# A batched matrix product on one core: the transposes of x in two pieces per half where there were four

## The chip, the core and the metric

The kernel runs on one core of one Trainium2 chip. Five engines work side by side and meet at semaphores: TensorE multiplies, VectorE, ScalarE and GpSimd copy and convert, SyncE (SP) starts the transfers between HBM and the on-chip memory (SBUF). Matrix products land in a second small memory (PSUM). The metric is the device time of the kernel in microseconds, lower is better. Before the change it is 132.26 us, the median of three runs from 132.15 to 132.43 us.

## The reference

```python
batch, dim_i, dim_j, dim_k = 32, 256, 512, 384
np.einsum('bij,bjk->bik', x, y).astype(np.float32)   # x: 32x256x512, y: 32x512x384, float32
```

Thirty-two independent products of a 256x512 matrix with a 512x384 matrix. Read are 16.8 MB of x and 25.2 MB of y, written are 12.6 MB.

## The kernel before, in words

The batches go in N = 8 groups of Q = 4. A group's four batches lie on four bands of 32 partitions each, and TensorE works on the bands as four tiles of 32 rows. One group's x is one load of 2 MB, its y one load of 3 MB, its output one store of 1.5 MB. x and y each have two buffers, so group n+2 is loaded into the place of group n.

- **SP** (lines 97 to 110) starts loads for groups 0 and 1 at once. Then, for n = 2 to 7, it waits until GpSimd has converted both halves of x of group n-2 and starts the load of x of group n; it waits for GpSimd's first half of x of group n-1 (by then y of group n-2 is converted too) and starts the load of y of group n. Only after the last load come the eight stores, in order, each behind a wait for the group's results; the last one waits for ScalarE's and VectorE's last copies. All transfers are in one queue.
- **GpSimd** (lines 118 to 133) converts x to 16 bits, half by half (a half e is four of the eight row blocks), then y in two or four pieces. Half e of x of group n waits for `s_free`, which VectorE raises with its first copy after a half's transposes; a piece of y waits until TensorE has used the piece that it overwrites.
- **VectorE** (lines 144 to 181) turns a half of x around into `xt_sb`, which holds one half at a time and is overwritten chunk by chunk. In `vector_half(n, e)` it transposes the half that comes next, while TensorE multiplies half (n, e): it waits for `chunk_done(n, e, a)`, TensorE's mark that chunk a of `xt_sb` has been read, and transposes piece a of the next half into that place. After the pieces it copies the last 5 of the half's 16 result blocks out of PSUM.
- **TensorE** (lines 220 to 240) does a half in 64 matmuls: 16 steps t, four bands each. `take` waits for a mark and takes it away. It takes one mark of `s_yr` and one of `s_xt` every four steps, which is once per chunk, and raises `s_pe` at each chunk's end.
- **ScalarE** (lines 185 to 199) copies the other 11 result blocks of each half.

The two halves of a group use different PSUM banks, so that TensorE can go on with one while the other is copied out. Nothing is planned by a scheduler: the order on every engine is that of the code.

Of the kernel before, what the change touches and what calls it, by code (L numbers as in the profile page):

```python
# [13 lines left out]
STEP = 4  # L14
# [4 lines left out]
def kernel(  # L19
# [14 lines left out]
    T = J // PQ  # L34
    TW = T // 2
    N = B // Q
    NC = T // STEP
# [21 lines left out]
    s_pe = nc.alloc_semaphore("s_pe")  # L59
# [27 lines left out]
    def chunk_done(n, e, a):  # L87
        return (n * NE + e) * MARKS + (a + 1 if a < NC - 1 else MARKS)
# [48 lines left out]


    v = nc.vector
    AW = STEP // 2  # L140
    words = x_r.bitcast(F32).rearrange("p e h (q t) -> p e t h q", t=TW)
    xt_w = xt_sb.rearrange("p t (h s) -> p t h s", s=PQ)

    def transpose_x(e, a):
        w = slice(a * AW, (a + 1) * AW)
        v.transpose(xt_w[:, w], words[:, e, w]).then_inc(s_xt, 1)  # L146
# [6 lines left out]
    def collect(copy, n, e, blocks, first=None, last=None):  # L153
        for i, (g, h) in enumerate(blocks):
            ins = copy(  # L155
                o_sb[g * PQ : (g + 1) * PQ, n, e, h],
                o_ps[h * PQ : (h + 1) * PQ, e * Q + g, :K],
            )
            if i == 0 and first is not None:
                ins.then_inc(first, 1)  # L160
            if i == len(blocks) - 1 and last is not None:
                ins.then_inc(last, 1)

    def vector_half(n, e):
        for a in range(NC):
            v.wait_ge(s_pe, chunk_done(n, e, a))
            if a == 0:
                v.wait_ge(s_cast, NE * n + e + 2)
            transpose_x(1 - e, a)
        collect(v.tensor_copy, n, e, BLOCKS[-OWN:], s_free, s_dve)  # L170

    v.sem_inc(s_dve, NE)
    v.wait_ge(s_cast, 1)
    for a in range(NC):
        transpose_x(0, a)
    with v.Fori(0, N - 1) as n:
        for e in range(NE):
            vector_half(n, e)
    vector_half(N - 1, 0)
    v.wait_ge(s_pe, chunk_done(N - 1, 1, NC - 1))  # L180
    collect(v.tensor_copy, N - 1, 1, BLOCKS[-OWN:], None, s_dve)
# [21 lines left out]
    def take(sem):  # L203
        te.wait_op(sem, 1, "sem-ge").then_inc(sem, -1)  # L204

    def product(ps, w, m, start, stop, g):
        return te.add_instruction(  # L207
            mybir.InstMatmult(
                name=nc.get_next_instruction_name(),
                start_tensor_calc=start,  # L210
                stop_tensor_calc=stop,
                tile_size=(PQ, P),
                tile_position=(PQ * g, 0),
                engine=mybir.EngineType.PE,
                ins=[te.lower_ap(m), te.lower_ap(w)],
                outs=[te.lower_ap(ps)],
            )
        )

    xt = xt_sb.bitcast(MM_DT).rearrange("p t (m c) -> p t m c", c=2)  # L220
    with te.Fori(0, N):
        with te.Fori(0, NE) as e:
            take(s_act)
            take(s_dve)
            for t in range(T):
                if t % STEP == 0:
                    take(s_yr)
                    take(s_xt)
                for g in range(Q):
                    s = slice(g * PQ, (g + 1) * PQ)  # L230
                    ins = product(
                        o_ps[:, e * Q + g, :K],
                        xt[s, t // 2, :, t % 2],
                        y_r[s, t],
                        t == 0,
                        t == T - 1,
                        g,
                    )
                    if t == T - 1 or (g == Q - 1 and t % STEP == STEP - 1):
                        ins.then_inc(s_pe, 1)  # L240
# [30 lines left out]
```

## Time and profile before

| | before |
|---|---|
| median of three runs | 132.26 us (132.15 to 132.43) |
| the profiled execution | 132.16 us, its span 130.8 us |
| busy VectorE / ScalarE / GpSimd | 82.7 / 84.3 / 74.2 us |
| busy TensorE matmul / weight load | 65.0 / 53.7 us |
| TensorE's mean granted clock | 0.798 |
| moved by DMA | 54.55 MB, mean 417 GB/s |
| transposes | 64, mean 625 ns |

Times in the profile count from the span's start. A row of the timeline names the start, the length, the engine, the line, the operation with the tile that it writes and reads, how many instructions are drawn together, and in brackets how long the engine had been idle and what ended that. `SPq` is SP's own instruction queue. The notes "<-DMA", "<-DVE" (VectorE), "<-POOL" (GpSimd) and "<-PE" (TensorE) name what a wait ended with.

### The profile page before, as it was taken

Reading aid. Unit: us, or ns where it says so; the run is one execution under the profiler, and the core shown is the slowest. Engines: PE = TensorE matmul, PEld = TensorE weight load, DVE = VectorE, ACT = ScalarE, POOL = GpSimd, SP = SyncE. Lnnn points to the kernel's source line nnn. Section 1 sums busy time; section 2 is a strip of 40 time slices with the busy share of each in tenths; the row PEclk is TensorE's granted clock in tenths of the full one; section 3 lists DMA queues with packets and bytes.
Section 4 is the critical chain, followed back from the end, with each engine's and each line's share of the span. In section 5 each row is a group of like instructions: output and inputs, shape, how many; then the busy total and the mean of one; then the engine's idle time right before and its main releaser. Section 6 shows DMA issues by size and latency. Waiting matters only on the chain. (4 is left out here: it accounts for less than half of the span.)

```text
span 130.8 us, 3204 instructions
## 1 busy us (share of the span) xinstructions
PE 65.0 (50%) x1024; PEld 53.7 (41%) x1024; DVE 82.7 (63%) x144; ACT 84.3 (64%) x178; POOL 74.2 (57%) x42
## 2 busy tenths in 40 slices
PE   0000069903991698099529915980985499100000
PEld 0000057702990575089329505970963387000000
DVE  0006005897379989966998997589989957920000
ACT  0400000899359989993999899489999967995000
POOL 0047195499919955992899469758964970000000
PEclk9999999996589779756986995599599558965555
DMA  5999999999999999999999999999999999999996
GB/s 105 421 461 406 426 433 466 406 423 436 458 393 431 433 466 398 421 438 458 396 456 413 458 391 453 413 431 421 458 413 405 427 427 428 432 425 428 436 425 263
DMA packets 3459, 54.55 MB, mean 417 GB/s; under 512 B 384, under 2 KB 384, under 8 KB 384
## 3 DMA queue, kind: packets, MB, share of 16 engines
q1 hardware_dynamic: 3456, 54.53, 98.2%
q14 instruction: 3, 0.02, 0.0%
HBM read 41.94 MB, written 12.58 MB: 417 GB/s over the span
## 5 line engine op out<-in xcount | busy, mean ns | idle before, releaser
L155 ACT COPY o_sb<-o_ps (+1 forms) x176 | 82.8, 470 | 31.7 <-PE o_ps L207 29.5
L207 PE MATMUL o_ps<-y_r,xt_sb 32*128 32x384 f16 x1024 | 65.0, 406 | 46.7 <-PEq L204 46.5
L207 PEld LDWEIGHTS o_ps<-y_r,xt_sb 32*128 32x128 f16 x1024 | 53.7, 112 | 57.7 <-issue 52.2
L146 DVE STREAM_TRANSPOSE xt_sb<-x_r 128x256 f32<-128x256 f32 x64 | 38.2, 625 | 31.0 <-PE o_ps L207 20.3
L132 POOL CAST y_r<-y_sb 128x1536 f16<-128x1536 f32 (+1 forms) x22 | 44.3, 2049 | 8.0 <-DMA y_sb<-in_y_dram 7.8
L155 DVE COPY o_sb<-o_ps 32x384 f32 (+1 forms) x80 | 44.5, 557 | 1.6
L124 POOL CAST x_r<-x_sb 128x2048 f16<-128x2048 f32 x16 | 30.2, 1893 | 24.6 <-PE o_ps L207 8.3
L192 ACT ACT_TABLE_LOAD x1 | 1.3, 1283 | 3.5 <-PEq L77 3.5
L255 POOL MEMSET const-float32-0.0<- 128x1 f32 x1 | 0.1, 98 | 0.2 <-issue 0.2
L192 ACT COPY spare<-const-float32-0.0 1x1 f32<-1x1 f32 x1 | 0.2, 190 | 0.0
L255 POOL MEMSET const-bfloat16-1.0<- 128x1 bf16 x1 | 0.1, 101 | 0.0
L255 POOL MEMSET const-uint8-127<- 128x1 uint8 x1 | 0.1, 101 | 0.0
L255 POOL MEMSET const-float32-1.0<- 128x1 f32 x1 | 0.1, 98 | 0.0
## 6 DMA issues: line engine op xcount, KB each, us to landing
y_sb<-in_y_dram SPq DMA_DIRECT2D x8, 3072.0 KB, 16.9
x_sb<-in_x_dram SPq DMA_DIRECT2D x8, 2048.0 KB, 17.4
out_dram<-o_sb SPq DMA_DIRECT2D x8, 1536.0 KB, 24.6
```

The lines of the kernel that those rows point to most:

```text
L124: po.tensor_copy(x_r[:, e], x_sb[n % 2][:, e * H : (e + 1) * H]).then_inc(s_cast, 1)
L132: ins = po.tensor_copy(y_r[:, s], y_sb[n % 2][:, s])
L146: v.transpose(xt_w[:, w], words[:, e, w]).then_inc(s_xt, 1)
L155: ins = copy(o_sb[g * PQ : (g + 1) * PQ, n, e, h], o_ps[h * PQ : (h + 1) * PQ, e * Q + g, :K],)
L192: a_.copy(spare, nc.const_aps.tensor(0.0, [1, 1], F32))
L207: return te.add_instruction(mybir.InstMatmult(name=nc.get_next_instruction_name(), start_tensor_calc=start, stop_tensor_calc=stop, tile_si ...
L255: nc = _bacc.Bacc("TRN2", target_bir_lowering=False, num_devices=1)
```

## The change

A half of x is transposed by two instructions of 128 partitions x 512 words, where it was four of 256 words. VectorE waits for TensorE's chunk 1 ahead of the first piece and for chunk 3 ahead of the second (before: for each of the chunks 0 to 3 ahead of its own piece). TensorE takes a mark of `s_xt` at steps 0 and 8 of a half, where it was 0, 4, 8 and 12. Marks of y, the marks that TensorE raises and all else stay as they are. Two lines more stand in the file, so line 146 becomes 147, 155 becomes 156, and TensorE's 207 becomes 208.

```diff
     v = nc.vector
-    AW = STEP // 2
+    PT = 2
+    AW = TW // PT
...
     def vector_half(n, e):
-        for a in range(NC):
-            v.wait_ge(s_pe, chunk_done(n, e, a))
+        for a in range(PT):
+            v.wait_ge(s_pe, chunk_done(n, e, (a + 1) * NC // PT - 1))
             if a == 0:
                 v.wait_ge(s_cast, NE * n + e + 2)
             transpose_x(1 - e, a)
...
     v.wait_ge(s_cast, 1)
-    for a in range(NC):
+    for a in range(PT):
         transpose_x(0, a)
...
             for t in range(T):
                 if t % STEP == 0:
                     take(s_yr)
+                if t % (T // PT) == 0:
                     take(s_xt)
```

## The prediction

> **What bounds the kernel now.** I read the busy times first, and then the transfers, since their row in the page is full from end to end. These are the first part of the page, the second (40 slices of 3.27 us, tenths of the 16 DMA engines' time), the third, and the sixth (transfers by line: count, size, median time to landing).
>
> ```profile
> PE 65.0 (50%) x1024; PEld 53.7 (41%) x1024; DVE 82.7 (63%) x144; ACT 84.3 (64%) x178; POOL 74.2 (57%) x42
> ...
> DMA  5999999999999999999999999999999999999996
> ...
> q1 hardware_dynamic: 3456, 54.53, 98.2%
> ...
> y_sb<-in_y_dram SPq DMA_DIRECT2D x8, 3072.0 KB, 16.9
> x_sb<-in_x_dram SPq DMA_DIRECT2D x8, 2048.0 KB, 17.4
> out_dram<-o_sb SPq DMA_DIRECT2D x8, 1536.0 KB, 24.6
> ```
>
> The one queue fills 98.2% of the span. No compute engine comes near that; the busiest, ScalarE, has 84.3 of 130.8 us. So the question is not what an engine saves but whether the queue ever waits for a release. For that I read the timeline at the places where GpSimd starts on a y (the end of the y load, where the bracket says so):
>
> ```profile
> 0.74 0.38 SPq L68 DMA_DIRECT2D x_sb<-in_x_dram  x1
> 8.46 3.72 POOL L124 CAST x_r<-x_sb 128x2048 f16<-128x2048 f32 x2 [8.01 <-DMA x_sb<-in_x_dram]
> 15.74 5.70 POOL L132 CAST y_r<-y_sb 128x1536 f16<-128x1536 f32 x4 [3.56 <-DMA y_sb<-in_y_dram]
> ...
> 40.45 5.44 POOL L132 CAST y_r<-y_sb 128x3072 f16<-128x3072 f32 x2
> 49.72 1.89 POOL L124 CAST x_r<-x_sb 128x2048 f16<-128x2048 f32 x1 [2.00 <-DVE o_sb L155]
> 52.41 5.44 POOL L132 CAST y_r<-y_sb 128x3072 f16<-128x3072 f32 x2 [0.80 <-DMA y_sb<-in_y_dram]
> 62.54 1.90 POOL L124 CAST x_r<-x_sb 128x2048 f16<-128x2048 f32 x1 [2.86 <-PE o_ps L207]
> 64.59 5.44 POOL L132 CAST y_r<-y_sb 128x3072 f16<-128x3072 f32 x2 [0.16 <-issue]
> 73.76 1.89 POOL L124 CAST x_r<-x_sb 128x2048 f16<-128x2048 f32 x1 [1.89 <-DVE o_sb L155]
> 76.79 5.44 POOL L132 CAST y_r<-y_sb 128x3072 f16<-128x3072 f32 x2 [1.14 <-DMA y_sb<-in_y_dram]
> 86.66 1.89 POOL L124 CAST x_r<-x_sb 128x2048 f16<-128x2048 f32 x1 [2.59 <-PE o_ps L207]
> 88.93 5.70 POOL L132 CAST y_r<-y_sb 128x1536 f16<-128x1536 f32 x4 [0.38 <-DMA y_sb<-in_y_dram]
> 97.53 1.89 POOL L124 CAST x_r<-x_sb 128x2048 f16<-128x2048 f32 x1 [1.06 <-DVE o_sb L155]
> 101.35 5.70 POOL L132 CAST y_r<-y_sb 128x1536 f16<-128x1536 f32 x4 [1.92 <-DMA y_sb<-in_y_dram]
> ```
>
> y of groups 0, 3, 5 and 7 lands at 15.74, 52.41, 76.79 and 101.35: 12.22, 12.19 and 12.28 us per group. One group's 5120 KB arrive every 12.2 us, whatever the engines do; x is 2048 of these 5120 KB, 4.9 us. After 101.35 the eight stores take the 29.45 us left, 3.68 us each.
>
> Next, how far ahead of need the transfers are started: SP's rows, the stores' line (first and last start), the loads' time to landing, and SP's last wait (in total, times, longest).
>
> ```profile
> 26.69 0.33 SPq L72 DMA_DIRECT2D y_sb<-in_y_dram  x1
> 35.74 0.33 SPq L72 DMA_DIRECT2D y_sb<-in_y_dram  x1
> 84.10 0.33 SPq L72 DMA_DIRECT2D y_sb<-in_y_dram  x1
> ...
> L95 SPq DMA_DIRECT2D out_dram<-o_sb x8: 332/430/434, 84.5 to 119.4; - x8
> ...
> DMA to landing us min/median/max: 7.7/17.4/20.6
> ...
> SPq L110 <- SPq L110: 11.0, 1, 11.0
> ```
>
> The load of y of group 2 starts at 26.69. The transfer ahead of it, x of group 2, ends at 15.74 + 12.2 + 4.9 = 32.8: 6.1 us of work still queued, the least of all loads. For y of group 3 it is 45.0 - 35.74 = 9.3 us, for y of group 7 it is 88.93 + 4.9 - 84.10 = 9.7 us. The last store starts at 119.4, and the store ahead of it ends at 130.8 - 3.68 = 127.1: 7.7 us. A start needs a lead: the very first x landed 7.7 us after its start, with 4.9 us of transfer, so at most 2.8 us. What a release may be late without cost is then 3.3 us at y of group 2, 6.5 us or more at the later loads and 4.9 us at the last store.
>
> **The change part by part.** (1) The piece. Transposes as they stand (their group with its busy time; then least, median and longest ns), four in a row, and the one at the end of group 3's first half with the copy and the TensorE work around it:
>
> ```profile
> L146 DVE STREAM_TRANSPOSE xt_sb<-x_r 128x256 f32<-128x256 f32 x64 | 38.2, 625 | 31.0 <-PE o_ps L207 20.3
> ...
> L146 DVE STREAM_TRANSPOSE xt_sb<-x_r x64: 592/640/649, 10.4 to 108.9; 128x256 f32<-128x256 f32 x64
> ...
> 10.38 2.21 DVE L146 STREAM_TRANSPOSE xt_sb<-x_r 128x256 f32<-128x256 f32 x4 [10.38 <-POOL x_r L124]
> ...
> 55.60 8.20 PE L207 MATMUL o_ps<-y_r,xt_sb 32*128 32x384 f16 x128 [3.78 <-PEq L204]
> 61.24 0.65 DVE L146 STREAM_TRANSPOSE xt_sb<-x_r 128x256 f32<-128x256 f32 x1 [0.50 <-PE o_ps L207]
> 61.91 2.86 DVE L155 COPY o_sb<-o_ps 32x384 f32 x5
> ```
>
> No row shows 512 words in one instruction. Four of 256 in a row take 2.21 us, 0.55 each, against 0.64 alone. If the length costs nothing, a piece takes 0.64; if the instruction is twice one alone, 1.28. I take one alone and one directly behind it, 0.64 + 0.55 = 1.19, because the rows in a row show that almost all of a transpose repeats with its words. VectorE's total: 32 x 1.19 = 38.1 us against the sum of 64 that was 38.2; nothing gained or lost there.
>
> (2) The release, the one loss. VectorE waits for chunk 3 with half the work still to do, where one quarter was left. The last piece ends 1.19 - 0.64 = 0.55 us later behind TensorE's half (between 0 and 0.64), and with it the first copy, `s_free`, GpSimd's second half of x and what SP queues behind that. Behind the longer wait on VectorE stand its five copies; TensorE waits for their mark only two halves later, and SP for the last ones. In the first groups this makes the start at 26.69 later by 0.55 us against 3.3 us that are free: cost 0.
>
> (3) Does the lateness pile up? GpSimd's round runs from the start on y to the end of the next x half, with TensorE's half and VectorE's last piece inside. From the rows: 49.72 + 1.89 - 40.45 = 11.16 us for group 2, then 12.03, 11.06, 11.76 and 10.49 for groups 3 to 6. With 0.55 more, groups 3 and 5 (12.58 and 12.31) exceed the 12.2 us of the transfers. Carried through: group 2 starts on y at 41.00, group 3 at 52.71 (0.30 late), group 4 at 65.29 (0.70), group 5 at 76.90 (0.11), group 6 at 89.21 (0.28), and its round ends at 100.25, ahead of y of group 7 at 101.35. So no load is started more than 0.70 + 0.55 = 1.25 us later, where at least 6.5 us are free, and the tail begins on time: cost 0.
>
> (4) TensorE's marks. 32 of 64 takes go; what one costs no row shows, between 0 and the 0.2 us that TensorE waited for transposes in all. The new danger is the second half of a group, which starts as the first ends, with half its `xt_sb` still being written. The fastest half takes 3.17 us (below, the row of that wait and of that half):
>
> ```profile
> PE o_ps L207 <- DVE xt_sb L146: 0.2, 1, 0.2
> ...
> 96.76 3.17 PE L207 MATMUL o_ps<-y_r,xt_sb 32*128 32x384 f16 x64 [0.56 <-PEq L204]
> ```
>
> Step 8 comes 1.58 us in, the piece is there after 1.19 (1.28 at most). No wait, and if there were one, the 3.78 us that TensorE idled ahead of 55.60 cover it: cost 0.
>
> (5) The tail, where cover is least.
>
> ```profile
> 108.81 10.61 ACT L155 COPY o_sb<-o_ps 32x384 f32<-32x384 f32 x22 [2.12 <-PE o_ps L207]
> 109.61 5.72 DVE L155 COPY o_sb<-o_ps 32x384 f32<-32x384 f32 x10
> ```
>
> The last store follows ScalarE's 22 copies, which end at 119.42 and depend on TensorE's banks. VectorE's ten end at 115.33, with the change at 115.9: 3.5 us ahead. Cost 0.
>
> Sum: 132.16 + 0 = 132.16 us for the profiled execution. The median shown is 0.10 us above it; I predict 132.2.
>
> **The rivals.** *Slower: the release round becomes the period.* Speaking for it: two of five rounds already pass 12.2 us with the change. With d for what a piece adds, group 2 starts on y at 40.45 + d, and five rounds later (56.50 + 5 d) the tail is late by 6 d + 40.45 + 56.50 - 101.35 = 6 d - 4.4 us. The last store has 4.9 us free, so a loss of 0.26 us needs d = 1.6, a piece of 2.25 us. Should a long piece cost twice the doubled one, 2.56 us (d = 1.92), the tail is 7.1 us late and the time 132.16 + 2.2 = 134.4. Against it: the rows of four, which grow no faster than the words.
>
> *Slower: GpSimd is shut out while VectorE transposes.* Each longer piece would then hold up a cast by 0.55 more; with three casts in a round d becomes 0.55 + 1.65 = 2.2, the tail is 8.8 us late, the time 136.1. The x casts speak against it (least, median, longest):
>
> ```profile
> L124 POOL CAST x_r<-x_sb x16: 1889/1893/1895, 8.5 to 97.5; 128x2048 f16<-128x2048 f32 x16
> ```
>
> They differ by 6 ns, and the second pair of halves at 8.46 took 3.72 us with the transposes of 10.38 running beside it. [...]
>
> *Faster: fewer instructions disturb the transfers less.* Ahead of most compute, y of group 0 came in 15.74 - 8.46 = 7.28 us; three fifths of 12.2 are 7.32. The 0.04 us over 13 such stretches (8 groups of 5 MB, 12 MB of stores) would be 0.5 us, 131.6, were all engines' work free of charge. VectorE's transposes are an eighth of the engines' busy time, and their words stay: 0.06 us at the most. [...]
>
> *The change doesn't do what it says*: the code fixes the counts (32 transposes, 32 marks of x), so they can't come out otherwise; it has no chance of its own.
>
> **How the numbers follow.** What can be told from no change is about 0.2%, 0.26 us: the three runs lie 0.28 us apart. No change 0.81; the slow round 0.06, the lock 0.01, an unseen slowing 0.05: slower 0.12; faster 0.07. Range: below to 131.9 (the runs' spread and half of the 0.5), above to 132.7, which is 0.5 us for a part of the lateness uncovered; the cases beyond, 134.4 and 136.1, stay out with the rest at under 2 in 10.
>
> **What would show it.** Transposes: 32, mean 1.10 to 1.28. The queue still at 98%, y of group 7 still ending GpSimd's wait at 101.3 to 101.4, rounds of GpSimd 0.5 longer, SP's load starts 0 to 1.3 later, its last wait still near 11 us. I am wrong if a "9" falls in the DMA row, if GpSimd's start on the last y no longer waits for DMA, or if the last wait falls toward 6 us.

## The result

The changed kernel takes 132.70 us in the median of 22 runs (132.44 to 133.06), the kernel before 132.49 us in 22 runs beside them (132.28 to 132.30 beside the later experiments); the ratio is 1.0022 with a 95% interval from 1.0013 to 1.0031. That is a small loss, about 0.3 us (0.17 to 0.41 by the interval), where the prediction was no change. One of the six runs of experiment 4 was in a slower state of the core and is left out of the figures given for it.

The profiled execution took 132.54 us, 0.38 us more than the profiled one of before. Its span is 130.8 us, the same as before. So these two differ only in what lies around the span: 1.36 us before, 1.74 us after. The page of the changed kernel (busy times, the DMA row in 40 slices, the queues):

```profile
PE 65.2 (50%) x1024; PEld 52.1 (40%) x1024; DVE 79.0 (60%) x112; ACT 84.1 (64%) x178; POOL 74.1 (57%) x42
...
DMA  5999999999999999999999999999999999999996
...
q1 hardware_dynamic: 3456, 54.53, 98.3%
q14 instruction: 2, 0.02, 0.0%
```

The transfers are as full as they were. One row differs that I had not read: queue 14 fetches instructions, and it moved two packets in the span. The page of the kernel before has three:

```profile
q14 instruction: 3, 0.02, 0.0%
```

The timeline of the changed kernel, at the places that the prediction named: SP's start of the load of y of group 2, GpSimd's starts on y of groups 2 to 7, VectorE's last copies.

```profile
27.24 0.33 SPq L72 DMA_DIRECT2D y_sb<-in_y_dram  x1
...
41.17 5.44 POOL L132 CAST y_r<-y_sb 128x3072 f16<-128x3072 f32 x2
52.47 5.44 POOL L132 CAST y_r<-y_sb 128x3072 f16<-128x3072 f32 x2
64.84 5.44 POOL L132 CAST y_r<-y_sb 128x3072 f16<-128x3072 f32 x2
76.89 5.44 POOL L132 CAST y_r<-y_sb 128x3072 f16<-128x3072 f32 x2 [0.68 <-DMA y_sb<-in_y_dram]
89.03 5.70 POOL L132 CAST y_r<-y_sb 128x1536 f16<-128x1536 f32 x4
101.56 5.70 POOL L132 CAST y_r<-y_sb 128x1536 f16<-128x1536 f32 x4 [1.70 <-DMA y_sb<-in_y_dram]
113.33 2.84 DVE L156 COPY o_sb<-o_ps 32x384 f32<-32x384 f32 x5 [0.34 <-PE o_ps L208]
```

And there the lines of the transposes and of the stores (least, median and longest ns, first and last start), and SP's last wait (in total, times, longest):

```profile
L147 DVE STREAM_TRANSPOSE xt_sb<-x_r x32: 1058/1104/1119, 10.5 to 109.0; 128x512 f32<-128x512 f32 x32
```

```profile
L95 SPq DMA_DIRECT2D out_dram<-o_sb x8: 332/430/439, 84.6 to 119.5; - x8
```

```profile
SPq L110 <- SPq L110: 10.9, 1, 10.9
```

Where the changed kernel lacks a fetch is seen in the stretch from 104 to 130 us (queue: packets, MB, share of 16 engines). The kernel before:

```profile
q1 hardware_dynamic: 1008, 10.92, 98.9%
q14 instruction: 1, 0.01, 0.1%
```

The changed kernel, with no row of queue 14 in the same stretch:

```profile
q1 hardware_dynamic: 1008, 10.92, 98.8%
```

### The profile page after: what moved, and what is told of

Same layout as the page of the kernel before. It is cut to its first block, busy times and chain, and to the rows that moved or that the text cites. A ratio compares the mean times of both kernels' runs of the same rounds, so it can differ in the third digit from the quotient of the medians.

```text
span 130.8 us, 3112 instructions
## 1 busy us (share of the span) xinstructions
PE 65.2 (50%) x1024; PEld 52.1 (40%) x1024; DVE 79.0 (60%) x112; ACT 84.1 (64%) x178; POOL 74.1 (57%) x42
## 3 DMA queue, kind: packets, MB, share of 16 engines
q1 hardware_dynamic: 3456, 54.53, 98.3%
## 5 line engine op out<-in xcount | busy, mean ns | idle before, releaser
L208 PEld LDWEIGHTS o_ps<-y_r,xt_sb 32*128 32x128 f16 x1024 | 52.1, 112 | 60.8 <-issue 55.3
L147 DVE STREAM_TRANSPOSE xt_sb<-x_r 128x512 f32<-128x512 f32 x32 | 34.5, 1096 | 35.2 <-PE o_ps L208 24.3
```

The source lines that it names most:

```text
L208: return te.add_instruction(mybir.InstMatmult(name=nc.get_next_instruction_name(), start_tensor_calc=start, stop_tensor_calc=stop, tile_si ...
```

## The experiments

Two theories stood against each other. A: the loss lies outside the span and comes from the length of VectorE's instruction stream, which went from 70 to 58 instructions. B: it lies inside, and comes from the longer pieces or the marks. Every run carries its time and its span (to 0.1 us), so the difference, called "outside" below, is a measurement of its own; a figure for it is the mean over the runs. A fetch is a packet of queue 14 of 8192 bytes, and a page is the stretch of instructions that one fetch brings. The counts of instructions are those of the stream as it stands in memory, where a loop's body counts once; the traces bear out the steps between them (VectorE's records hold 67 different instructions of before and 55 of the changed kernel, also 12 apart; experiment 3 has 12 instructions more at its waits).

**1. The kernel before, again.**

```diff
-    AW = STEP // 2
+    AW = STEP // 2  # words of t per piece
```

> The kernel before with a comment added and nothing else; it gives the spans of runs of the kernel before, of which only one is known (132.16 us with a span of 130.8, so 1.36 us outside). Theory A (the loss lies outside the span): the spans are those of the changed kernel, on the mean 131.0, and 1.3 to 1.4 us lie outside where the changed kernel has 1.67 to 1.76. Theory B (the loss lies inside the span, lost in the transfers): the spans are 0.2 to 0.3 us shorter than those of the changed kernel, about 130.75, and as much lies outside as there. Both: ratio to the kernel before 1.000.

Measured: 132.29 us, ratio 1.0000 (0.9991 to 1.0010). The mean span is 131.01 us, that of the 22 runs of the changed kernel is 131.01 us too. Outside lie 1.33 us here (1.28 to 1.38 in 12 runs) and 1.72 us there (1.67 to 1.76 in 22). The two do not overlap. So the loss lies outside the span, 0.39 us by these means, and B is left with nothing that shows.

**2. TensorE's marks alone, with four pieces.**

```diff
-        v.transpose(xt_w[:, w], words[:, e, w]).then_inc(s_xt, 1)
+        ins = v.transpose(xt_w[:, w], words[:, e, w])
+        if a % 2 == 1:
+            ins.then_inc(s_xt, 1)
...
-                    take(s_xt)
+                if t % (2 * STEP) == 0:
+                    take(s_xt)
```

> The kernel before with TensorE's part alone: VectorE keeps its four pieces and gives a mark with the second and the fourth, TensorE takes two marks per half. VectorE has the 70 instructions of the kernel before in its stream, TensorE has two fewer than before. Theory A in the form that VectorE's shorter stream makes the loss: 132.2 to 132.6, ratio 1.000, 1.3 to 1.4 outside. In the form that TensorE's shorter stream makes it: ratio 1.002 with 1.7 outside. Theory B (longer pieces): ratio 1.000.

Measured: 132.37 us, ratio 1.0002 (0.9989 to 1.0014), outside 1.33, three fetches in the span. Neither the missing takes nor a stream of TensorE that is two instructions shorter cost or gain anything that shows.

**3. Both parts of the change, with VectorE's stream filled up to 70.**

```diff
     v.wait_ge(s_cast, 1)
+    for _ in range(24):
+        v.wait_ge(s_cast, 1)
     for a in range(PT):
         transpose_x(0, a)
```

(In the built program the 24 waits stand as 12 instructions.)

> The changed kernel, with idle waits put on VectorE ahead of its first transposes (they are already met there and end microseconds before TensorE needs anything), so that its stream has the 70 instructions of the kernel before where the change left 58. Theory A (length of VectorE's stream): ratio 1.000, 1.3 to 1.4 us outside the span. Theory B (two long pieces cost inside): ratio 1.002 as the changed kernel.

Measured: 132.34 us, ratio 1.0000 (0.9988 to 1.0011), outside 1.33, mean span 131.02. From its page:

```profile
q14 instruction: 3, 0.02, 0.0%
...
L147 DVE STREAM_TRANSPOSE xt_sb<-x_r 128x512 f32<-128x512 f32 x32 | 34.5, 1097 | 34.8 <-PE o_ps L210 22.8
```

The transposes are those of the changed kernel, 32 of 1.1 us; the third fetch is back in the span, and the loss is gone. The change as it works on the data costs nothing that these runs can tell (the interval is 0.12% to either side).

**4. One piece, filled up to 70.**

```diff
-    PT = 2
+    PT = 1
...
+    for _ in range(36):
+        v.wait_ge(s_cast, 1)
```

> One piece of 1024 words per half and one mark, VectorE's stream again at 70 instructions. The release comes about 2.1 - 0.64 = 1.5 us later per half than before, where the change made it 0.5. Theory A: the same time as before or within 0.1 us, since 6 x 1.5 - 4.4 = 4.6 us of lateness at the tail stays under the 4.9 us that I had free; 1.3 to 1.4 outside. Theory B: the loss inside the span grows with the delay, from 0.3 to about 0.9 us, ratio near 1.007.

Measured: 139.72 us (138.62 to 140.27 in five runs), ratio 1.0572 (1.0544 to 1.0600), outside 1.37. My sum for this run was wrong by far. Its DMA row, its timeline and the line of its stores show why:

```profile
DMA  5999999999999999999999999999989999977328
```

```profile
52.91 4.38 PE L210 MATMUL o_ps<-y_r,xt_sb 32*128 32x384 f16 x64 [2.44 <-PEq L207]
57.41 2.03 DVE L147 STREAM_TRANSPOSE xt_sb<-x_r 128x1024 f32<-128x1024 f32 x1 [1.92 <-PE o_ps L210]
59.75 4.37 PE L210 MATMUL o_ps<-y_r,xt_sb 32*128 32x384 f16 x64 [2.46 <-PEq L207]
```

```profile
L95 SPq DMA_DIRECT2D out_dram<-o_sb x8: 332/380/432, 91.1 to 132.2; - x8
```

With one piece nothing of the next half can be transposed while TensorE works, and TensorE waits for the whole transpose each time. A half takes 59.75 - 52.91 = 6.84 us and a group 13.7, over the 12.2 us of the transfers. This loop of TensorE and VectorE is not the one through GpSimd that I had summed. The DMA row (slices of 3.43 us) falls for good only in slice 36, at 120 us, with one 8 ahead of it: the loads kept their pace though, from y of group 3 on, each load of y was started with less in hand than the one before (the starts lie 13.3 to 13.7 us apart), and the whole loss falls on the last stores, the last of which starts at 132.2 instead of 119.4. So the free time at the loads and the tail is real, and it is used up by 1.5 us per group.

**5. The changed kernel, again, on one chip with experiments 6, 7 and 8.**

```diff
-    PT = 2
+    PT = 2  # pieces per half
```

> The changed kernel with a comment added and nothing else, on one chip with the three that follow. Theory A: its loss lies outside the span again, 1.7 us there against 1.3 to 1.4 of the kernel before, spans alike at 131.0, two instruction fetches in the span; 132.65 to 132.75. Theory B is out by the run with idle waits; it would have the spans differ.

Measured: 132.71 us beside 132.28 of the kernel before, ratio 1.0023 (1.0010 to 1.0036), outside 1.74 against 1.33, two fetches in the span.

**6. Filled up to 70 at the end of the stream.**

```diff
     collect(v.tensor_copy, N - 1, 1, BLOCKS[-OWN:], None, s_dve)
+    for i in range(12):
+        v.memset(idle[:, i : i + 1], 0.0)
```

(`idle` is a new tensor of 1 x 12.)

> The changed kernel with 12 small writes on VectorE behind its last copy, so that its stream has 70 instructions, with nothing changed ahead of the last transposes. Theory A1 (a page of VectorE's instructions is fetched after the last store, unless the stream reaches far enough to have it fetched earlier): a third fetch in the span again, 1.3 to 1.4 us outside, 132.3. Theory A2 (it is where the loop lies in its page that matters, which these writes do not move): 1.7 outside, 132.7.

Measured: 132.28 us, ratio 1.0005 (0.9992 to 1.0018), outside 1.33, three fetches. Here nothing ahead of VectorE's last copy is moved, neither the loop nor its place; A2 is out. What counts is how far the stream reaches.

**7. and 10. Filled up to 64, and to 61.** The edit is that of experiment 3 with 12 and with 6 waits.

> The changed kernel with half the idle waits, VectorE's stream at 64 instructions. Theory A1 has a step somewhere between 58 and 70, so either 1.7 outside and two fetches in the span, or 1.35 and three; nothing between. A rival (each instruction on VectorE less costs outside in proportion): about 1.55 outside, 132.5.

> The changed kernel with idle waits up to 61 instructions on VectorE. It halves the stretch from 58 to 64 in which the step lies: 1.7 outside and 132.7, or 1.35 and 132.3, and nothing between.

Measured: with 64 instructions 132.25 us, ratio 0.9995 (0.9981 to 1.0009), outside 1.34, three fetches. With 61, 132.51 us, ratio 1.0014 (1.0002 to 1.0026), outside 1.49 (1.45 to 1.52 in 10 runs), two fetches. "Nothing between" was wrong: 61 lies between, at 1.49. But it is not a proportion either, since 64 and 70 are alike (1.34 and 1.33). Between 58 and 61 each instruction is worth (1.72 - 1.49) / 3 = 0.08 us, and past 64 nothing. The packets of queue 14 in the traces tell when the third fetch starts: at 106.6 us in the kernel before, 106.3 in experiment 3, 112.5 in experiment 6 and 124.7 with 64 instructions; with 61 and with 58 there is none up to the end of the span. So it comes later as VectorE's stream is cut, and as long as it falls in the span it costs nothing. That fits a fetch which falls behind the last store with 61 and 58 instructions and is waited for there, but it is argued and not shown. The steps are not even either: with 64 the fetch starts 9 us after VectorE's last copy has ended (115.6), and what asks for it there the runs do not tell.

**8. and 9. The kernel before, four pieces and all, with 116 and with 122 small writes on VectorE.**

```diff
     v.sem_inc(s_dve, NE)
+    for i in range(60):
+        v.memset(idle[:, i : i + 1], 0.0)
...
     collect(v.tensor_copy, N - 1, 1, BLOCKS[-OWN:], None, s_dve)
+    for i in range(60, 116):
+        v.memset(idle[:, i : i + 1], 0.0)
```

(The other run has 122 in place of 116.)

> The kernel before, four pieces and all, with 116 small writes on VectorE, 60 of them ahead of its first work and 56 behind its last, all in time in which it is idle. [...] Theory A1: 1.7 outside, ratio 1.002 to 1.003, although no piece and no wait differs from before. Rival (a longer stream is simply better, or the length has nothing to do with pages): 1.35 outside, ratio 1.000.

> As the run with 116 small writes on VectorE, with six more of them behind its last copy: 192 instructions, which is 64 + 128. If the place of the stream's end in a page of 128 instructions decides, this one is to the run with 116 what 64 instructions were to 58: 1.3 to 1.4 us outside the span, and a fourth fetch in the span (three, and the one at 9.6 us that the longer stream brought), and 132.5 us in all. If 116 writes cost by their number, it is no faster than that run: 1.7 outside, 132.9.

Measured: with 116 writes (186 instructions) outside 1.71, with 122 (192 instructions) outside 1.32. So four pieces show the loss too when the stream ends 128 instructions further than that of the changed kernel, and six writes more take it away. The place of the stream's end decides in these runs, and it comes back after 128 instructions (1.72 us with 58, 1.71 with 186; 1.34 with 64, 1.32 with 192), with one fetch more in the span; the pieces have no part in it. (A period of 64 would fit these runs too, but not the one fetch more for 128 instructions.) That it would come back there, which the 1.7 us expected with 186 instructions rests on, was an assumption of mine that no run ahead of these showed.

The whole times did not come out as I wrote: 132.93 us, ratio 1.0042 (1.0028 to 1.0056), and 133.03 us, ratio 1.0052 (1.0039 to 1.0066), because the spans grew, to means of 131.25 and 131.72 us where the kernel before has 131.0. In the run with 116: the queues over the whole span, then in the stretch from 9 to 10.5 us, and the end of the first y load.

```profile
q14 instruction: 3, 0.02, 0.0%
```

```profile
q14 instruction: 1, 0.01, 1.3%
```

```profile
16.42 5.70 POOL L133 CAST y_r<-y_sb 128x1536 f16<-128x1536 f32 x4 [4.17 <-DMA y_sb<-in_y_dram]
```

The longer stream brought a fetch into the first load of y, where it takes 1.3% of 16 engines over 1.5 us, which is 0.31 us on one engine. That load ends at 16.42 where it was 15.74 (at most 15.95 in the other nine profiles without that fetch). In the run with 122 there is that fetch and one in the tail as well, at 124.2 us, close to the 124.7 with 64 instructions:

```profile
q14 instruction: 4, 0.03, 0.1%
```

```profile
16.38 4.29 POOL L133 CAST y_r<-y_sb 128x1536 f16<-128x1536 f32 x3 [4.02 <-DMA y_sb<-in_y_dram]
```

The lateness of y, 0.64 us, is about the 0.7 us by which its mean span grew. In the run with 116 the profiled execution, whose y is 0.68 us late, has a span of 131.5 us, but the mean over the six runs grew by 0.2 only; why, the runs do not tell. That the fetch makes the load late is argued too: both profiles that have it show the lateness, the x ahead of that y landed on time (GpSimd starts on it at 8.53 and 8.63, where it starts at 8.46 before and at 8.54 in the changed kernel), and the 60 early writes had ended at 5.9 us. But the fetch holds one engine for only half as long as the load is late.

All of it in one table; the instructions are those of VectorE's stream, the outside is the mean over the runs.

| kernel | pieces | instructions | fetches in the span | mean span, us | outside, us | median, us |
|---|---|---|---|---|---|---|
| before (27 runs beside experiments 5 to 8) | 4 | 70 | 3 | 131.04 | 1.33 | 132.28 |
| marks alone | 4 | 70 | 3 | 131.06 | 1.33 | 132.37 |
| changed | 2 | 58 | 2 | 131.01 | 1.72 | 132.70 |
| changed, again (experiment 5) | 2 | 58 | 2 | 130.91 | 1.74 | 132.71 |
| changed, to 61 | 2 | 61 | 2 | 131.01 | 1.49 | 132.51 |
| changed, to 64 | 2 | 64 | 3 | 130.99 | 1.34 | 132.25 |
| changed, to 70, ahead | 2 | 70 | 3 | 131.02 | 1.33 | 132.34 |
| changed, to 70, at the end | 2 | 70 | 3 | 131.05 | 1.33 | 132.28 |
| before and 116 writes | 4 | 186 | 3, one of them at 9.6 us | 131.25 | 1.71 | 132.93 |
| before and 122 writes | 4 | 192 | 4, one of them at 9.5 us | 131.72 | 1.32 | 133.03 |

What is shown: the loss is outside the span, it follows the length of VectorE's stream and nothing else of the change, it comes back 128 instructions further, and each time it is there, one fetch near the end of the span is missing. What is inferred: that the missing fetch takes place behind the last store and that VectorE's end waits for it. No profile here reaches behind the span. Ahead of it the traces have five to seven fetches, with no tie to the loss (six before, seven in the changed kernel, six in the changed kernel again). The sizes fit: up to 1.72 - 1.33 = 0.39 us are lost, and a fetch holds one engine for 0.31 us.

Inside the span the fetch near its end shows nothing: with it (experiment 3) the mean span is 131.02 us, without it (the changed kernel) 131.01 us.

## Why the prediction was wrong

The time: predicted 132.2 us, in a range from 131.9 to 132.7, with 0.81 for no change. Measured 132.70, slower by 0.22%. By its own steps:

- **What bounds the kernel** was right. The DMA row is the same digit by digit, the queue has 98.3% where it had 98.2%, and the mean span did not move (131.01 us, and 131.01 in experiment 1).
- **(1) The piece.** I took 1.19 us between 0.64 and 1.28; it is 1.10, so the row of four (0.55 each) was the better price than a mixture. VectorE's sum fell from 38.2 to 34.5 us where I had 38.1. It changed nothing.
- **(2) The release** came later, as predicted, and cost nothing. Its size agrees by luck: y of group 2 is started at 27.24, 0.55 us later, but the same two kernels profiled again (experiments 1 and 5) have 26.08 and 26.48, and with the piece as measured the term is 1.10 - 0.64 = 0.46 us.
- **(3) The piling up.** Predicted starts on y were 41.00, 52.71, 65.29, 76.90, 89.21 and, on time, 101.35; the rows have 41.17, 52.47, 64.84, 76.89, 89.03 and 101.56, where GpSimd still waits 1.70 us for the transfer. GpSimd's lateness stays at 0.72 us or less and does not grow. Its rounds, from these starts to the ends of the next x halves, grew by 0.10 to 0.41 us, where I had 0.55 for each (these x casts of 1.89 us start at 50.54, 63.00, 74.32, 87.17 and 97.97).
- **(4) TensorE's marks** cost nothing that shows: experiment 2 has the ratio 1.0002, and in experiment 3, with the two marks and the long pieces, it is 1.0000.
- **(5) The tail.** VectorE ends at 113.33 + 2.84 = 116.17 (predicted 115.9), the last store starts at 119.5 as before, SP's last wait is 10.9 us instead of 11.0.
- **The sum** is the step that failed: "132.16 + 0 = 132.16 us for the profiled execution". I summed what the change does in the span and carried the 1.36 us around the span over as a constant. It is a term of its own, which the sum put at no change without a reason, and the change moved it to 1.74 us by shortening VectorE's stream by 12 instructions. The row that bears on it, queue 14, stood in the page of before, though that row alone gives neither where a page ends nor the price.
- **The rivals.** The slow round did not come with two pieces, and its formula was wrong besides: with one piece (experiment 4) it gave no loss, and over 7 us were lost, through a loop of TensorE and VectorE that it does not contain. GpSimd was not shut out either ("the lock" of the chances): beside the long transposes GpSimd's casts of x take 1889 to 1894 ns, as before (1889 to 1895). "Fewer instructions disturb the transfers less" brought no gain, the mean span being the same; fewer instructions cost, by another way. Its sum was off besides: 52 MB of loads and stores are 17 stretches of 3 MB, not 13, and would have made 0.7 us of its 0.5. What happened fell under the 0.05 for an unseen slowing.

## What to carry to other kernels

Here one queue filled the span from end to end (98.2% and 98.3%), and an edit on VectorE, busy for 60% of it, still had a way to the time: through what lies around the span. In such a kernel take the time outside the span as a term of its own, compare it first when a small difference turns up, and look at the instruction queue's row: here 12 instructions fewer moved that time by 0.4 us, and 6 to 12 idle ones more took that away again, at the start or at the end of the stream. Before such a difference is put down to the edit, fill the stream up to its old length and measure once more.

## What the runs showed of the hardware that was not expected

- In these runs the time outside the span depends on where VectorE's stream ends, and the place comes back after 128 instructions: 1.32 to 1.34 us with 64, 70 or 192 instructions, 1.49 with 61, 1.71 to 1.74 with 58 and 186. The mechanism behind it is inferred.
- One fetch of instructions among full transfers may delay a load by more than it lasts: in the two profiles with a fetch at 9.5 to 9.6 us the first y ended at 16.42 and 16.38 where it ended at 15.74, though the fetch holds one of 16 engines for 0.31 us. That the fetch alone does it is not shown; the fetch at 106.6 us stands among full transfers too, and the mean span is 131.0 us with it and without it.
- A transpose of 512 words takes 1.10 us where two of 256 words on their own take 1.28, and one of 1024 takes 2.03: the words are most of the price, with about 0.2 us per instruction beside them, an estimate from these times (2 x 1.10 - 2.03 = 0.17).
